# Layer norm's mean held to an upper place in TensorE's order, and layer 0's output projection begun with attention's half for two pairs of features

## The chip, the cores and the metric

The kernel runs on one core of one Trainium2 chip. The metric is the device time of one execution in microseconds (us); the time before is the median of three runs, 1300.79 us (1300.74 to 1301.24). The trace comes from one further execution, 1300.42 us long, of which the instructions span 1298.6 us. The engines are TensorE (PE: products, its weight loads are PEld), VectorE (DVE), ScalarE (ACT), GpSimd (POOL) and SyncE (SP, which issues most loads). They run their own queues in order and meet by semaphores.

## The reference, cut to what matters

A two-layer trunk works on 384 tokens (128 of a prompt, 256 of a sample) of 2048 features. Layer 0 is the one that changes:

```
h    = rms_norm(x, g) * (1 + sc) + sh             # sc, sh, gate: c @ w_mod
ga, gb, gate_a, q, k, v, gate_b = split(h @ w_in)
a = ga * sigmoid(gb)
a = depthwise_conv(a, conv_w) + conv_b            # 31 taps
a = silu(layer_norm(a, ln_g, ln_b)) * silu(gate_a)        # 1024 features
b = attention(norm(q), norm(k), v) * silu(gate_b)         # 1024 features
x = x + gate * (concat([a, b]) @ w_out)                   # 2048 x 2048
```

The layer norm goes over the 1024 features of `a`: it needs the mean over them, then the variance of what is left. Layer 1 (windowed attention beside a short gated convolution) follows, and a last RMS norm.

## The kernel before

Activations lie with features on the partitions: `mix` holds 16 tiles of 128 features by 384 tokens, tiles 0 to 7 for the convolution's half `a`, tiles 8 to 15 for attention's half `b`. Every matrix is multiplied in three products of split numbers: high x high, high x low, low x high. For that ScalarE casts a tile to its high part (`hhi` for activations, `whi` for weights, both at L283) and VectorE subtracts it for the low part (`hlo`, `wlo`, L284).

`proj_feat` (L394) makes one *pair* of feature tiles: two PSUM accumulators, over two units of 8 input tiles each. `feat_unit` (L374) runs one unit: two *halves* of 4 input tiles, each with its own weight load (512 KB on SyncE's queue), its split, and 24 products (L382) of 128x128 by 128x384. There are 5 accumulators (`pf`), 2 auxiliary PSUM buffers (`aux`: attention's `s_ps`, `pT_ps`, `o_ps`, the layer norm's `mean`, `rsl`, `rbl`), 6 raw weight buffers, and 3 each for `whi` and `wlo`.

The order in each engine's queue is set by a list scheduler that goes by a timeline of its own, within data dependencies and the few manual ones. A manual dependency of the kind NOSYNC says only that one instruction stands behind another on the same engine.

The end of layer 0, in the order of the program: attention; four pairs of `gate_a`; four pairs of `gate_b` (L781 to L797). After the first pair of `gate_b`, `ln_mean` (L751) sums the eight convolution tiles over the features with one product of TensorE (`mean`, L757), and `ln_center` subtracts it and gathers the squares (`lvar`). After the second pair `rsl` (L240) sums the squares over features, VectorE takes the inverse root (L229 to L234), TensorE spreads it (`rbl`, L256), `ln_out` multiplies (L773) and applies SiLU on ScalarE (L774). Last, L799 multiplies the result into tiles 0 to 7 of `mix`, and `out_proj` (L569) splits all 16 tiles and runs eight pairs (L588), tiles 0 to 7 before tiles 8 to 15 in each. The last two pairs are *held*: both do tiles 0 to 7, then both do the rest. Beside all this VectorE computes 64 dot products for layer 1's modulation rows (L207), whose operand `area` GpSimd's queue loads (L91) into buffers that are attention's until it ends.

Of the kernel before, what the change touches and what calls it, by code (L numbers as in the profile page):

```python
# [17 lines left out]
NOSYNC = mybir.DependencyInfo(mybir.DependencyClass.NoSync, mybir.DependencyReason.DATA)  # L18
# [4 lines left out]
T = 384  # L23
# [28 lines left out]
def trunk(ctx: ExitStack, tc: tile.TileContext, d: dict, o: dict):  # L52
# [10 lines left out]
    def aux(name):  # L63
        return ps_aux.tile([P, 512], F32, tag="aux", name=name)

    def acc(name):
        return ps_acc.tile([P, 512], F32, tag="acc", name=name)
# [24 lines left out]
        if order["hold"] is not None:  # L92
            tc.add_manual_dep(ins, order["hold"].name, SYNC, reason="side loads wait")

    order = {"last": None, "split": None, "hold": None}

    def sync_load(dst, src):
        ins = nc.sync.dma_start(dst, src).ins
# [4 lines left out]
    def load_w(w, k0, nk, f0, nf, raw=None):  # L103
        if raw is None:
            raw = wp.tile([P, nk, nf], F32, tag="raw", name="raw")
        sync_load(raw, w[:, k0:k0 + nk, f0:f0 + nf])
        return raw
# [174 lines left out]
    def split(dst_hi, dst_lo, src):  # L282
        nc.scalar.copy(dst_hi, src)  # L283
        order["split"] = nc.vector.tensor_tensor(dst_lo, src, dst_hi.bitcast(F32), ALU.subtract).ins  # L284

    def make_h(layer, k):
        if layer == 1:
            h = tmp.tile([P, T], F32, tag="wk", bufs=4, name="h1")
            for g, c0, c1 in GROUPS:
                nc.scalar.activation(h[:, c0:c1], x["T"][:, k, c0:c1], AF.Copy, scale=mods[layer, 1][:, k, g:g + 1])  # L290
            split(hhi[:, k, :T], hlo[:, k, :T], h)
            return
        for g, c0, c1 in GROUPS:
            a = mods[layer, 1][:, k, g:g + 1]
            nc.scalar.activation(hhi[:, k, c0:c1], x["T"][:, k, c0:c1], AF.Copy, scale=a)  # L295
            nc.vector.scalar_tensor_tensor(hlo[:, k, c0:c1], x["T"][:, k, c0:c1], a, hhi[:, k, c0:c1].bitcast(F32),
                                           ALU.mult, ALU.subtract)
# [20 lines left out]
    def pump():  # L318
        bg["due"] += bg["rate"]
        while bg["due"] >= 1.0 - 1e-6 and gemv_q:  # L320
            bg["due"] -= 1.0
            gemv_q.pop(0)()
# [23 lines left out]
    def load_split(w, k0, nk, nf):  # L346
        raw = load_w(w, k0, nk, 0, nf)
        hi = wp.tile([P, nk, nf], F32R, tag="whi", name="whi", bufs=NHI)
        lo = wp.tile([P, nk, nf], F32R, tag="wlo", name="wlo", bufs=NLO)
        split(hi, lo, raw)  # L350
        return hi, lo
# [22 lines left out]
    def feat_unit(pp, w, u, n, begin, end):  # L374
        for hf in range(2):
            hi, lo = load_split(w, 8 * u + 4 * hf, 4, 256)
            for j in range(2):
                fj = slice(j * P, (j + 1) * P)
                for i in range(4):
                    k = 8 * u + 4 * hf + i  # L380
                    for m, (x, y) in enumerate(((hi, hhi), (hi, hlo), (lo, hhi))):
                        ins = nc.tensor.matmul(pp[j][:, :n], lhsT=x[:, i, fj], rhs=y[:, k, :n],  # L382
                                               start=(begin and k % 8 == 0 and m == 0),
                                               stop=(end and k % 8 == 7 and m == 2)).ins
                        order["product"] = ins
            for _ in range(FILL):
                if fill_q:
                    fill_q.pop(0)()
        pump()

    def pair():
        return [acc(f"pf{j}") for j in range(2)]

    def proj_feat(w, evac, units=(0, 1), n=T):  # L394
        pp = pair()
        for u in units:
            feat_unit(pp, w, u, n, u == units[0], u == units[1])
        for j in range(2):
            evac(j, pp[j])
# [166 lines left out]
            return go  # L566
        return ev

    def out_proj(layer, w, mix, units, each, split_last=0, between=None):  # L569
        gate = mods[layer, 2]  # L570
        for k in (*range(8 * units[0], 8 * units[0] + 8), *range(8 * units[1], 8 * units[1] + 8)):
            split(hhi[:, k, :T], hlo[:, k, :T], mix[:, k, :])

        def ev(fb):
            def go(j, ps):
                f = 2 * fb + j
                if layer == 0:
                    s = tmp.tile([P, T], F32, tag="wk", bufs=4, name="go")
                    for g, c0, c1 in GROUPS:
                        nc.scalar.activation(s[:, c0:c1], ps[:, c0:c1], AF.Copy, scale=gate[:, f, g:g + 1])  # L580
                    nc.vector.tensor_tensor(x["T"][:, f, :], x["T"][:, f, :], s, ALU.add)
                else:
                    for g, c0, c1 in GROUPS:
                        nc.vector.scalar_tensor_tensor(x["T"][:, f, c0:c1], ps[:, c0:c1], gate[:, f, g:g + 1],
                                                       x["T"][:, f, c0:c1], ALU.mult, ALU.add)
                each(f)
            return go
        for fb in range(8 - split_last):  # L588
            proj_feat(w[fb], ev(fb), units)
        held = {fb: pair() for fb in range(8 - split_last, 8)}  # L590
        for fb, pp in held.items():
            feat_unit(pp, w[fb], units[0], T, True, False)
        if between:
            between()
        for fb, pp in held.items():
            feat_unit(pp, w[fb], units[1], T, False, True)
            for j in range(2):
                ev(fb)(j, pp[j])


    w0 = d["wf0"]
# [18 lines left out]
    for j, nf in enumerate(widths):  # L620
# [7 lines left out]
        last = j == len(widths) - 1  # L628
# [36 lines left out]
    mix = big.tile([P, KC, T], F32, tag="bigB", name="mix0")  # L665
# [85 lines left out]
    def ln_mean():  # L751
        av = tmp.tile([P, T], F32, tag="sacc", name="lsum", bufs=1)
        nc.vector.tensor_tensor(av, apad[:, 0, :T], apad[:, 1, :T], ALU.add)
        for c in range(2, 8):
            nc.vector.tensor_tensor(av, av, apad[:, c, :T], ALU.add)
        pm = aux("mean")
        ins = nc.tensor.matmul(pm[:, :T], lhsT=ones.broadcast_to([P, P]), rhs=av, start=True, stop=True).ins  # L757
        tc.add_manual_dep(ins, order["product"].name, NOSYNC, reason="not before its place")
        ln["m"] = tmp.tile([P, T], F32, tag="rb", name="mean", bufs=1)
        nc.scalar.activation(ln["m"], pm[:, :T], AF.Copy, scale=1.0 / CW)  # L760

# [20 lines left out]
    for fb in range(4):  # L782
        proj_feat(w0[12 + fb], evb(2 * fb))
        if fb == 0:
            ln_mean()
            for c in range(8):
                ln_center(c)
        if fb == 1:
            drain(gemv_q)
            ring["slots"] = []  # L790
            x["T"] = big.tile([P, KC, T], F32, tag="bigA", name="xT2")
            side_load(x["T"], d["xT"])
            ln["r"] = rstd_rows(rstd_cols([ln["v"]], CW, "rsl", order["product"]), "rbl")
            for c in range(8):
                ln_out(c)
            shifts.append(mod_rows(1, 0, 3, vring, ln["out"]))
            scales = [mod_rows(1, 1, j, vring, ln["out"]) for j in (1, 2, 3)]  # L797
# [5 lines left out]
    def each(f):  # L803
        square(f)
        if f in SCALE_AT:
            scales.pop(0)()
            if f == SCALE_AT[1]:
                for done in shifts:
                    done()
    def ahead():  # L810
        drain(gemv_q)
        for k in range(8):
            make_h(1, k)
    out_proj(0, d["w_out0"], mix, (0, 1), each, 2, ahead)


    for k in range(8, KC):
# [6 lines left out]
    mix = big.tile([P, KC, T], F32, tag="bigB", name="mix1")  # L824
# [101 lines left out]
    def each(f):  # L926
# [8 lines left out]
        if f % 4 == 1 and f > 4:  # L935
            q = f // 4 - 1
            nc.scalar.copy(y[0][:, 0, 512 * q:512 * q + 512], y_block(q, 0, after=False))
    out_proj(1, d["w_out1"], mix, (1, 0), each)
    rs2 = rstd_cols([av, *tail], D, "rs2")
    mid = [y_block(q, 1, acc) for q in range(3)]  # L940
# [96 lines left out]
```

## Time and profile before

| what | us |
|---|---|
| median of three runs | 1300.79 |
| the profiled execution | 1300.42 |
| its span of instructions | 1298.6 |
| TensorE busy | 1257.6 |
| VectorE busy | 884.9 |
| ScalarE busy | 564.6 |

The span is read as one chain: work that ended last, followed back to what released it. A row of a timeline gives start and duration; where an engine sat idle before, the bracket names who ended the wait. Products overlap in the array, so a product's duration is about twice the distance to the next; the sums go by the distance. The names in a row are the program's, without buffer numbers.

### The profile page before, as it was taken

To read this page: it belongs to the slowest core of one execution; us is meant where nothing else is said; L and a number is where in the kernel's file an instruction comes from. 1 tells how busy PE (TensorE), PEld (TensorE's weight loads), DVE (VectorE), ACT (ScalarE), POOL (GpSimd) and SP (SyncE) were. 2 spreads that over 40 slices of the span, in tenths; PEclk is the share of its full clock that TensorE was granted. 3 is DMA by queue.
4 is the path that set the end of the run, shared out by engine and by line. 5 is a ranking of instruction groups with operands and counts; after the bars stand their busy time and mean duration, and the time that the engine had idled before them with its cause. 6 is when DMAs were issued, how large, how long until landed. Compare 5 with 4: busy or idle time off the path is not lost.

```text
span 1298.6 us, 17795 instructions
## 1 busy us (share of the span) xinstructions
PE 1257.6 (97%) x6856; PEld 1116.1 (86%) x6856; DVE 884.9 (68%) x1507; ACT 564.6 (43%) x989; POOL 96.3 (7%) x137
## 2 busy tenths in 40 slices
PE   6999999999999999599999999999999999999997
PEld 3566676888978799499999988899999999999997
DVE  2244688998989975999976942354443599994443
ACT  3345432664465655433464632254444423343322
POOL 0211100000000000111100000000000011101110
PEclk9999999999999999799999999999999999999999
DMA  9989987787554344387743444333333578844422
GB/s 367 401 305 356 342 318 289 301 321 250 188 201 146 116 163 154 108 266 255 251 155 119 129 130 125 120 120 115 100 97 106 166 259 271 267 148 129 130 65 97
DMA packets 67620, 257.97 MB, mean 199 GB/s; under 512 B 7056, under 2 KB 11408, under 8 KB 59984
## 3 DMA queue, kind: packets, MB, share of 16 engines
q1 hardware_dynamic: 54736, 203.51, 45.4%
q0 software_dynamic: 12656, 53.23, 12.0%
q8 instruction: 53, 0.87, 0.3%
q14 instruction: 31, 0.25, 0.1%
q10 hardware_dynamic: 144, 0.10, 0.0%
HBM read 253.15 MB, written 3.67 MB: 198 GB/s over the span
## 4 chain that ended last, share of the span: by engine, by line
PE 96%; DVE 2%; DMA 1%; ACT 0%; issue 0%; SPq 0%; DVEq 0%; ACTq 0%
PE pf L382 68%; PE pt L361 10%; PE q L612 6%; PE gv L139 5%; PE s_ps L505 2%; PE o_ps L530 2%; PE pT_ps L526 1%; DMA ring<-in_mod_w 1%; PE y_ps L921 1%; PE gv L172 0%; PE qT_ps L491 0%; PE gv L676 0%; DVE mix L799 0%; DVE apad L773 0%; DVE area L207 0%
## 5 line engine op out<-in xcount | busy, mean ns | idle before, releaser
L382 PE MATMUL pf<-hhi,whi 128*128 128x384 f32 (+1 forms) x1664 | 568.9, 342 | 10.9 <-ACT hhi L283 10.6
L382 PE MATMUL pf<-hlo,whi 128*128 128x384 f32 (+1 forms) x1664 | 570.9, 343 | 5.0 <-DVE hlo L284 5.0
L382 PE MATMUL pf<-hhi,wlo 128*128 128x384 f32 (+1 forms) x1664 | 565.7, 342 | 1.2 <-DVE wlo L284 1.2
L284 DVE TENSOR_TENSOR wlo<-raw,whi 128x1024 fp32r<-128x1024 f32 x256 | 313.0, 1224 | 285.5 <-ACT whi L283 280.6
L283 ACT CAST whi<-raw 128x1024 fp32r<-128x1024 f32 x256 | 268.3, 1050 | 475.1 <-PE pf L382 267.4
L382 PEld LDWEIGHTS pf<-hhi,whi 128*128 128x128 f32 x1664 | 313.6, 189 | 31.9 <-issue 14.6
L382 PEld LDWEIGHTS pf<-hhi,wlo 128*128 128x128 f32 x1664 | 313.7, 189 | 12.2 <-issue 4.7
L382 PEld LDWEIGHTS pf<-hlo,whi 128*128 128x128 f32 x1664 | 314.1, 189 | 10.8 <-DVE hlo L284 5.5
L207 DVE CUSTOM_DVE_ANT_0 area<-area,crow 128x1024 f32<-128x1024 f32 x128 | 151.3, 1218 | 4.9 <-PE o_ps L530 4.4
L702 DVE SCALAR_TENSOR_TENSOR cv<-apad,cw,cv 128x399 f32<-128x399 f32 x240 | 138.7, 628 | 0.0
L361 PE MATMUL pt<-wlo,hhi 128*128 128x512 f32 x192 | 75.8, 395 | 0.0
L361 PE MATMUL pt<-whi,hhi 128*128 128x512 f32 x192 | 75.4, 396 | 0.0
L361 PE MATMUL pt<-whi,hlo 128*128 128x512 f32 x192 | 74.1, 395 | 0.0
L91 POOL DMA_DIRECT2D area<-in_modT x64 | 33.9, 531 | 457.6 <-DVE sm L207 223.8
L276 POOL TENSOR_TENSOR sacc<-sacc,sqf 128x384 f32<-128x384 f32 x28 | 33.5, 1196 | 176.4 <-ACT sqf L275 175.6
L361 PEld LDWEIGHTS pt<-whi,hhi 128*128 128x128 f32 x192 | 36.0, 188 | 11.0 <-ACT hhi L308 1.7
L612 PE MATMUL q<-whi,hhi 128*128 128x512 f32 x96 | 41.1, 428 | 4.4 <-ACT hhi L295 4.4
L361 PEld LDWEIGHTS pt<-whi,hlo 128*128 128x128 f32 x192 | 35.9, 188 | 10.0 <-DVE wlo L284 1.7
L139 PE MATMUL gv<-ring,cst 128*32 128x512 f32 (+1 forms) x288 | 35.6, 582 | 8.6 <-DMA ring<-in_mod_w 7.7
L361 PEld LDWEIGHTS pt<-wlo,hhi 128*128 128x128 f32 x192 | 36.1, 188 | 9.1 <-issue 0.8
L513 ACT ACTIVATE pr<-s_ps,nm 128x384 f32<-128x384 f32 (+1 forms) x48 | 24.4, 509 | 44.2 <-DVE nm L512 34.4
L612 PE MATMUL q<-wlo,hhi 128*128 128x512 f32 x96 | 40.5, 422 | 0.0
(186 smaller groups left out, 1005.9 us busy)
## 6 DMA issues: line engine op xcount, KB each, us to landing
raw<-in_wf SPq DMA_DIRECT2D x144, 512.0 KB, 4.5
ring<-in_mod_w SPq DMA_DIRECT2D x32, 1024.0 KB, 7.0
raw<-in_w_out SPq DMA_DIRECT2D x64, 512.0 KB, 4.1
area<-in_modT POOLq DMA_DIRECT2D x64, 512.0 KB, 5.2
lent<-in_mod_w SPq DMA_DIRECT2D x20, 1024.0 KB, 4.9
raw<-in_wq SPq DMA_DIRECT2D x32, 512.0 KB, 8.7
raw<-in_wt SPq DMA_DIRECT2D x24, 512.0 KB, 3.6
lent<-in_modT POOLq DMA_DIRECT2D x8, 1024.0 KB, 8.2
```

The source lines that it names most:

```text
L91: ins = nc.gpsimd.dma_start(dst, src).ins
L139: nc.tensor.matmul(ps[32 * g:32 * g + 32, :nf], lhsT=stat(k), rhs=raw[:, i % raw.shape[1], :], start=(k < 4), stop=(k >= KC - 4))
L207: ins = nc.vector.tensor_tensor_reduce(out=raw if g else junk, in0=raw, in1=crow[:, g, h * n:(h + 1) * n], scale=1.0, scalar=0.0, op0=ALU. ...
L276: eng.tensor_tensor(av, av, s, ALU.add)
L283: nc.scalar.copy(dst_hi, src)
L284: order["split"] = nc.vector.tensor_tensor(dst_lo, src, dst_hi.bitcast(F32), ALU.subtract).ins
L361: nc.tensor.matmul(pp[t], lhsT=x[:, k, tt], rhs=y[:, i, :], start=(k == 0 and n == 0), stop=(k == KC - 1 and n == 2))
L382: ins = nc.tensor.matmul(pp[j][:, :n], lhsT=x[:, i, fj], rhs=y[:, k, :n], start=(begin and k % 8 == 0 and m == 0), stop=(end and k % 8 == ...
L505: nc.tensor.matmul(ps, lhsT=mix[:, h0 + h, t * P:(t + 1) * P], rhs=kT[:, kv, c0:c0 + nk * P], start=True, stop=True)
L530: nc.tensor.matmul(po, lhsT=v[:, slots[j], kv * HD:(kv + 1) * HD], rhs=pT[:, j, :], start=(j == 0), stop=(j == nk - 1))
L612: nc.tensor.matmul(pq[b][t], lhsT=x[:, k, tt], rhs=y[:, 0, 512 * b:512 * b + 512], start=(k == 0 and n == 0), stop=(k == KC - 1 and n == 2))
L702: nc.vector.scalar_tensor_tensor(st["o"], apad[:, c, j:j + CVW], cw[:, c, j:j + 1], st["o"], ALU.mult, ALU.add)
```

## The change

`order` gets two entries: a count of halves issued, and a mark `must`. `ln_mean` now sets the mark: the product of the mean has to stand in front of the first product of the fifth half behind it, that is in front of the third pair of `gate_b`. In `out_proj` the code for held pairs becomes a function, `by_halves`, which is also used at the beginning (`split_first`). Layer 0 calls it with units (1, 0): tiles 8 to 15 first. So the first two pairs both do attention's half (8 halves of weights in the first four of which only tiles 8 to 15 are read), then both do the convolution's half; pairs 2 to 5 go tiles 8 to 15, then 0 to 7; the last two, with the units turned round, stay as they were. The sums and the products are the same.

```diff
--- before.py
+++ after.py
@@ -92,7 +92,7 @@
         if order["hold"] is not None:
             tc.add_manual_dep(ins, order["hold"].name, SYNC, reason="side loads wait")
 
-    order = {"last": None, "split": None, "hold": None}
+    order = {"last": None, "split": None, "hold": None, "must": None, "halves": 0}
 
     def sync_load(dst, src):
         ins = nc.sync.dma_start(dst, src).ins
@@ -374,6 +374,7 @@
     def feat_unit(pp, w, u, n, begin, end):
         for hf in range(2):
             hi, lo = load_split(w, 8 * u + 4 * hf, 4, 256)
+            order["halves"] += 1
             for j in range(2):
                 fj = slice(j * P, (j + 1) * P)
                 for i in range(4):
@@ -382,6 +383,9 @@
                         ins = nc.tensor.matmul(pp[j][:, :n], lhsT=x[:, i, fj], rhs=y[:, k, :n],
                                                start=(begin and k % 8 == 0 and m == 0),
                                                stop=(end and k % 8 == 7 and m == 2)).ins
+                        if order["must"] and order["must"][1] == order["halves"]:
+                            tc.add_manual_dep(ins, order["must"][0].name, NOSYNC, reason="not behind this place")
+                            order["must"] = None
                         order["product"] = ins
             for _ in range(FILL):
                 if fill_q:
@@ -566,7 +570,7 @@
             return go
         return ev
 
-    def out_proj(layer, w, mix, units, each, split_last=0, between=None):
+    def out_proj(layer, w, mix, units, each, split_first=0, split_last=0, between=None):
         gate = mods[layer, 2]
         for k in (*range(8 * units[0], 8 * units[0] + 8), *range(8 * units[1], 8 * units[1] + 8)):
             split(hhi[:, k, :T], hlo[:, k, :T], mix[:, k, :])
@@ -585,17 +589,21 @@
                                                        x["T"][:, f, c0:c1], ALU.mult, ALU.add)
                 each(f)
             return go
-        for fb in range(8 - split_last):
+
+        def by_halves(fbs, units, between=None):
+            held = {fb: pair() for fb in fbs}
+            for fb, pp in held.items():
+                feat_unit(pp, w[fb], units[0], T, True, False)
+            if between:
+                between()
+            for fb, pp in held.items():
+                feat_unit(pp, w[fb], units[1], T, False, True)
+                for j in range(2):
+                    ev(fb)(j, pp[j])
+        by_halves(range(split_first), units)
+        for fb in range(split_first, 8 - split_last):
             proj_feat(w[fb], ev(fb), units)
-        held = {fb: pair() for fb in range(8 - split_last, 8)}
-        for fb, pp in held.items():
-            feat_unit(pp, w[fb], units[0], T, True, False)
-        if between:
-            between()
-        for fb, pp in held.items():
-            feat_unit(pp, w[fb], units[1], T, False, True)
-            for j in range(2):
-                ev(fb)(j, pp[j])
+        by_halves(range(8 - split_last, 8), units[::-1], between)
 
 
     w0 = d["wf0"]
@@ -756,6 +764,7 @@
         pm = aux("mean")
         ins = nc.tensor.matmul(pm[:, :T], lhsT=ones.broadcast_to([P, P]), rhs=av, start=True, stop=True).ins
         tc.add_manual_dep(ins, order["product"].name, NOSYNC, reason="not before its place")
+        order["must"] = (ins, order["halves"] + 5)
         ln["m"] = tmp.tile([P, T], F32, tag="rb", name="mean", bufs=1)
         nc.scalar.activation(ln["m"], pm[:, :T], AF.Copy, scale=1.0 / CW)
 
@@ -811,7 +820,7 @@
         drain(gemv_q)
         for k in range(8):
             make_h(1, k)
-    out_proj(0, d["w_out0"], mix, (0, 1), each, 2, ahead)
+    out_proj(0, d["w_out0"], mix, (1, 0), each, 2, 2, ahead)
 
 
     for k in range(8, KC):
```

What the scheduler makes of it, at three places. On TensorE, at the end of attention 0: the last query block's transposes (`pT_ps`), its output (`o_ps`) and the layer norm's `mean`, among the products of the second pair of `gate_b` (`pf_3872` is the last accumulator of it) and the third (`pf_4146`, `pf_4147`). Before, around the mean:

```order
L382 MATMUL pf_4146<-hhi,whi 128x384
L382 MATMUL pf_4146<-hlo,whi 128x384
L382 MATMUL pf_4146<-hhi,wlo 128x384
L530 MATMUL o_ps<-pT,kv 128x512
L757 MATMUL mean<-lsum,ones 128x384
L382 MATMUL pf_4147<-hhi,whi 128x384
L382 MATMUL pf_4147<-hlo,whi 128x384
L382 MATMUL pf_4147<-hhi,wlo 128x384
```

In the change, at the same product of `pf_3872` as before:

```order
L383 MATMUL pf_3872<-hlo,whi 128x384
L383 MATMUL pf_3872<-hhi,wlo 128x384
L530 MATMUL pT_ps<-ident,pr 128x128 x12
L534 MATMUL o_ps<-pT,kv 128x512 x3
L765 MATMUL mean<-lsum,ones 128x384
L383 MATMUL pf_4146<-hhi,whi 128x384
L383 MATMUL pf_4146<-hlo,whi 128x384
L383 MATMUL pf_4146<-hhi,wlo 128x384
```

The mean moves up by 65 rows, to the front of the third pair; since it takes one of the two auxiliary buffers in turn, the attention rows that use them earlier (12 transposes and 3 products of `o_ps`, before strewn among the products down to the mean) move up with it. Then come 85 products up to `rsl`, 38 from there to `rbl`, and 69 from `rbl` to the output projection.

On VectorE, from the layer norm's multiplication by the inverse root (`apad<-apad,rb`) to the splits of `mix` into low parts. `ISA area` and `ISA sm` are one dot product for layer 1. Before:

```order
L773 TENSOR_TENSOR apad<-apad,rb 128x384 x8
L565 TENSOR_TENSOR mix_1217<-mix_1217,sg 128x384
L207 ISA area,sm_4046<-area,crow 128x1024
L207 ISA sm_4046 128x1
L284 TENSOR_TENSOR hlo<-mix_1217,hhi 128x384 x3
L799 TENSOR_TENSOR mix_1217<-mix_1217,apad 128x384 x7
L207 ISA area,sm_4046<-area,crow 128x1024
L207 ISA sm_4046 128x1
L207 ISA area,sm_4046<-area,crow 128x1024
L207 ISA sm_4046 128x1
L799 TENSOR_TENSOR mix_1217<-mix_1217,apad 128x384
L284 TENSOR_TENSOR hlo<-mix_1217,hhi 128x384 x8
```

In the change:

```order
L782 TENSOR_TENSOR apad<-apad,rb 128x384 x8
L207 ISA area,sm_4046<-area,crow 128x1024
L207 ISA sm_4046 128x1
L808 TENSOR_TENSOR mix_1217<-mix_1217,apad 128x384 x4
L284 TENSOR_TENSOR wlo<-raw,whi 128x1024
L808 TENSOR_TENSOR mix_1217<-mix_1217,apad 128x384
L207 ISA area,sm_4046<-area,crow 128x1024
L207 ISA sm_4046 128x1
L207 ISA area,sm_4046<-area,crow 128x1024
L207 ISA sm_4046 128x1
L808 TENSOR_TENSOR mix_1217<-mix_1217,apad 128x384 x3
L284 TENSOR_TENSOR hlo<-mix_1217,hhi 128x384 x5
```

The multiplication, the dot products and the products into `mix` stand as they did; a weight split has come between, the gate product is gone from here to a later place, and the first row of `hlo` in the change holds attention's tiles 8, 9 and 10 and the convolution's 0 and 1. Behind these 12 rows follow `wlo`, three `hlo` (tiles 11, 2, 3), two dot products, the gate product of tile 14, and `hlo` of tiles 12, 13 and 4.

On TensorE, where the output projection begins (`pf_4443` and `pf_4444` are its first pair, `pf_4445` and `pf_4446` its second). Before:

```order
L382 MATMUL pf_4275<-hlo,whi 128x384
L382 MATMUL pf_4275<-hhi,wlo 128x384
L256 MATMUL rbl<-diag,ones 128x128 x3
L382 MATMUL pf_4443<-hhi,whi 128x384
L382 MATMUL pf_4444<-hhi,whi 128x384
L382 MATMUL pf_4443<-hlo,whi 128x384
L382 MATMUL pf_4443<-hhi,wlo 128x384
L382 MATMUL pf_4443<-hhi,whi 128x384
```

In the change, nine products into the projection:

```order
L383 MATMUL pf_4443<-hhi,wlo 128x384
L383 MATMUL pf_4443<-hhi,whi 128x384
L383 MATMUL pf_4444<-hlo,whi 128x384
L383 MATMUL pf_4444<-hhi,wlo 128x384
L383 MATMUL pf_4444<-hhi,whi 128x384
L383 MATMUL pf_4445<-hhi,whi 128x384
L383 MATMUL pf_4445<-hlo,whi 128x384
L383 MATMUL pf_4446<-hhi,whi 128x384
L383 MATMUL pf_4446<-hlo,whi 128x384
```

Before, `rbl` is the last thing in front of the projection, and the first pair stands alone; in the change the first 96 products are those of two pairs on tiles 8 to 15, mixed. SyncE's loads and GpSimd's queue stand in the same order as before, but for the output stores at the very end.

## Rows read from the trace of the kernel before

**Rows 1.** TensorE's waits over the span: engine, line, releaser: us, times, longest.
```profile
PE pf L382 <- ACT hhi L283: 10.6, 1, 10.6
...
PE pf L382 <- DVE hlo L284: 5.0, 1, 5.0
```

**Rows 2.** Timeline of TensorE from 481 us: start, duration, engine, line, operation, count, idle before.
```profile
482.21 0.34 PE L382 MATMUL pf<-hhi,whi 128*128 128x384 f32 x1
...
521.10 0.93 PE L256 MATMUL rbl<-diag,ones 128*128 128x128 f32 x6
532.65 1.01 PE L382 MATMUL pf<-hhi,whi 128*128 128x384 f32 x2 [10.62 <-ACT hhi L283]
538.61 0.69 PE L382 MATMUL pf<-hlo,whi 128*128 128x384 f32 x1 [4.96 <-DVE hlo L284]
...
541.66 0.39 PE L382 MATMUL pf<-hlo,whi 128*128 128x384 f32 x1
```

**Rows 3.** Timeline of VectorE (DVE), 478 to 545 us, columns as in Rows 2.
```profile
498.00 3.84 DVE L763 TENSOR_TENSOR apad<-apad,mean 128x384 f32<-128x384 f32 x8 [2.00 <-ACT mean L760]
...
514.25 0.15 DVE L246 TENSOR_SCALAR rsl<-rsl 128x3 f32<-128x3 f32 x1
...
515.44 0.16 DVE L232 TENSOR_TENSOR nt<-ny 128x3 f32<-128x3 f32 x1
...
520.75 0.68 DVE L255 TENSOR_SCALAR diag<-ident,rsl 128x128 f32<-128x128 f32 x3
522.18 1.23 DVE L284 TENSOR_TENSOR wlo<-raw,whi 128x1024 fp32r<-128x1024 f32 x1 [0.75 <-ACT whi L283]
...
524.73 3.83 DVE L773 TENSOR_TENSOR apad<-apad,rb 128x384 f32<-128x384 f32 x8
...
528.95 1.22 DVE L207 CUSTOM_DVE_ANT_0 area<-area,crow 128x1024 f32<-128x1024 f32 x1
...
537.54 3.83 DVE L284 TENSOR_TENSOR hlo<-mix,hhi 128x384 fp32r<-128x384 f32 x8
```

**Rows 4.** Chain of waits, 480 to 545 us: start, us until the next link, link.
```profile
490.98 0.44 PE pT_ps L526 x4
491.41 1.72 PE o_ps L530 x4
...
496.80 0.65 PE mean L757 x2
497.44 15.60 PE pf L382 x89
513.04 0.56 PE rsl L240 x6
```

**Rows 5.** Windows: busy time of PE, PEld, DVE, ACT, POOL; granted clock; DMA share; GB/s.
```profile
14.00:18.00 4.00, 3.03 (x7) 2.45 (x8) 2.93 (x7) 1.65 (x5) 0.00 (x0) 1.00 1.11 350
...
48.00:50.00 2.00, 2.00 (x7) 1.54 (x6) 1.15 (x4) 0.30 (x1) 0.00 (x0) 0.50 0.99 406
...
539.00:541.00 2.00, 2.00 (x7) 2.00 (x7) 2.00 (x6) 0.00 (x0) 1.65 (x1) 0.50 0.13 51
```

**Rows 6.** Timeline of ScalarE (ACT), 478 to 545 us, columns as in Rows 2.
```profile
481.12 2.14 ACT L521 ACTIVATE pr<-pr,den 128x384 f32<-128x384 f32 x4 [0.24 <-DVE den L519]
483.17 1.03 ACT L283 CAST whi<-raw 128x1024 fp32r<-128x1024 f32 x1
486.89 1.08 ACT L527 COPY pT<-pT_ps 128x512 f32<-128x512 f32 x2 [2.69 <-PE pT_ps L526]
```

**Rows 7.** Timeline of TensorE in the first stage, columns as in Rows 2.
```profile
14.97 0.79 PE L612 MATMUL q<-whi,hhi 128*128 128x512 f32 x1 [2.19 <-ACT hhi L295]
...
45.87 0.50 PE L612 MATMUL q<-whi,hhi 128*128 128x512 f32 x1 [2.20 <-ACT hhi L295]
```

**Rows 8.** Timeline of GpSimd (POOL), 420 to 545 us, columns as in Rows 2.
```profile
497.09 1.57 POOL L91 DMA_DIRECT2D area<-in_modT  x3 [46.31 <-PE o_ps L530]
```

**Rows 9.** The page: DMA issues, count, size, median us from issue to landing.
```profile
area<-in_modT POOLq DMA_DIRECT2D x64, 512.0 KB, 5.2
```

## The prediction, made before the run

> **What bounds the kernel now.** I read the page's chain first: TensorE carries nearly all of it, so time is gained only where TensorE stops or runs slowly. Its waits by releaser show where: in the middle of the kernel there are only two of note, 10.6 us on ScalarE's `hhi` and 5.0 us on VectorE's `hlo`, each a single wait [rows 1]. The timeline of TensorE puts both between the layer norm's broadcast at 521.10 and the output projection [rows 2]: two products begin at 532.65, the third at 538.61. Behind that TensorE runs to the last sums without a wait of note. The chain of waits there goes through VectorE: inverse root, eight multiplications at 524.73, dot products, products into `mix`, low parts [rows 3]. So the projection waits for the layer norm, whose tiles 0 to 7 it reads first, and the layer norm started at 498.00, when the mean was there [rows 3, 4].
>
> What the stop costs: six records of the broadcast take 0.56 us as the six of `rsl` do [rows 4], so products could go on at 521.66; 538.61 less 521.66 is 16.95, less two products done in between, 0.35, leaves 16.6. A product takes 15.60 / 89 = 0.175 us [rows 4]. After the stop nine steps take 541.66 - 538.61 = 3.05 us instead of 1.58 [rows 2]; the granted clock there is 0.50, the 1.2 GHz level [rows 5]. That adds 1.5. All that can go is 18.1 us.
>
> **The change part by part.** No instruction is added or taken away: all terms are places in queues.
>
> *The mean moves up, and attention's tail with it.* In both kernels the product of 482.21 [rows 2] is the first of the third gate pair. In the change 12 transposes, 3 products of `o_ps` and the mean stand in front of it: 3 x 0.44 + 3 x 0.86 + 0.65 = 4.55 us of work [rows 4], which before lay among the next 60 products. It cannot run through. The last softmax scaling ends at 483.2, and behind it on ScalarE a weight cast runs to 484.2 [rows 6]; only then come the copies of the transposes, 0.54 each [rows 6]. With two buffers the third group of transposes waits for the first copy, and `o_ps` for the second: 484.2 + 1.1 = 485.3. Then 2.6 for `o_ps`, 0.65 for the mean: 488.5. The gate products start 6.3 us later than before, 4.55 of which is work that is no longer in their way: **new idle 1.75 us**. Every gate product, its weight splits and their loads are queued behind it; three splits are ahead, so none runs dry.
>
> *The layer norm moves up.* The mean ends at 488.5 instead of 497.45. ScalarE first copies `o_ps`, then the mean, so centring starts at about 489.2 instead of 498.00. It and the squares share VectorE with two weight splits and end near 499.7. TensorE's place for `rsl` is 85 products behind the mean: 488.5 + 14.9 = 503.4, so the place decides, not the squares. `rsl` takes 0.56. Twelve small steps at 0.2 (seven of them stand between 514.25 and 515.44) and the diagonals' 0.7 [rows 3] end at 507.2; the broadcast's place, 38 products behind `rsl`, is 510.6. It ends at 511.2, its copy on ScalarE, taken like the copies of [rows 6], at 512.0. The eight multiplications start at **512.2 instead of 524.73: 12.5 us earlier**. The 69 products from the broadcast to the projection end at 511.2 + 12.1 = 523.2.
>
> *The projection starts with attention's half.* On VectorE's queue there stand, from 512.2: eight multiplications 3.75, a dot product 1.15, four products into `mix` 1.9, a weight split 1.15, one product 0.45, two dot products 2.3, three products 1.4 (distances from [rows 3]: 0.47 for 128x384, 1.15 for 128x1024). That is 12.1: 524.3. The low part of tile 8 is done at 524.85. TensorE has had two products that need only high parts and stood since 523.55: **wait 1.3 us**. It then has 28 products before the first that reads tile 12's low part: until 529.75. VectorE meanwhile does five low parts 2.35, a weight split 1.15, three low parts 1.4, two dot products 2.3, a gate product and tile 12's low part 1.0: 532.5. **Wait 2.75 us**. The other tiles of the first 96 products come in time, by my count with 0.1 us to spare at tile 14: the 96 end at 544.1. Before, product 97 began at 541.66 + 85 x 0.175 = 556.5. That is 12.4 us, and the balance of waits says the same: 18.1 - 1.75 - 1.3 - 2.75 = 12.3.
>
> *What is late next.* The layer norm's tiles are split by 537 and read from 544.1: the cover of 96 products holds. VectorE then has per half of 4.2 us one weight split and two dot products, 3.45 us, and about 0.5 for sums: it follows, as before, and all of its work moved with it. Of five accumulators the first pair and the last gate pair hold four, so one of the second pair's two comes free only when ScalarE has read the gate pair, some 2 us after its last product; about ten of the projection's products stand in front. Taken at nothing, bounds 0 and 1.
>
> *Loads.* SyncE's and GpSimd's queues keep their order. The `area` loads, which waited for attention's end at 497.09 [rows 8], can go 9 us earlier; they take 5.2 us [rows 9], and the dot products in front of tile 8 stand more than 20 us behind.
>
> *The clock.* Two waits of nearly one length on TensorE stand in the first stage, 2.19 us at 14.97 and 2.20 us at 45.87 [rows 7]. Behind the second the granted clock was 0.50 from 48 to 50; around the first it was 1.00, the 2.4 GHz level, from 14 to 18 [rows 5]. So my 2.75 us may or may not lower it, and if it does, 1.5 us are lost as after the old stop. I take none, since 28 products at full speed stand ahead of that wait; 1.5 stays in the range. [...]
>
> Sum: 1300.4 - 12.3 = 1288.1 for an execution like the profiled one. That one is 0.4 under the median shown, so I say **1288.3 us**.
>
> **Rivals.**
> - *The new waits throttle the clock.* For: 45.87 in [rows 7]. Against: 14.97 in the same rows. 1289.8 with one, 1291.3 with both.
> - *VectorE's queue becomes the bound by more than I counted.* Tile 12's low part stands behind two dot products and two weight splits, tile 14's behind four dot products; any late operand stops all that follow. For: in the sum above VectorE is never idle, and my spare time at tile 14 is 0.1 us. If the fourth load from the new order, issued when its buffer falls free, landed in 9 us instead of 5.2 [rows 9], or the chain began 3 to 4 us later, each would add that much: 1292.
> - *The cover is better than counted.* If ScalarE takes the attention copies ahead of time or VectorE's waits fall where TensorE has other pairs to do, the 5.8 us of new waits shrink; at nothing left, 1282.5. Against: the queues are in order, and the sums leave no choice.
> - *Slower.* One mechanism: TensorE, stopped at short intervals over the first two pairs, stays at 1.2 GHz for all of their 192 products. Each then costs 0.32 - 0.175 = 0.145 more: 27.8 us, less the 2.75 wait that slower products would hide: 1313. It decides from 85 products on, where the gain of 12.3 is eaten. Against: after 541.66 full distance came back in nine products, with VectorE just as far behind.
> - *That it doesn't do what it says* is shut out by the order: the mean stands 65 rows up, and tiles 8 to 15 are the first the projection reads.
>
> **How the numbers follow.** The forecast's own range, 1286.5 to 1289.5, has 0.5; the clock 0.2; VectorE's queue 0.13; better cover 0.1; the slow clock 0.03; what I overlooked 0.04, half of it within 0.2% of before (what a measurement of this kernel can tell from no change: 1298.2 to 1303.4). The range goes from 1285 (half of the better cover) to 1293 (all but the worst of VectorE's case). Faster 0.93, same 0.04, slower 0.03.
>
> **What would show it.** Right: the mean's product ends near 488.5, centring starts near 489, the eight multiplications near 512; TensorE's wait on `hhi` is gone, and on `hlo` there are one of 1 to 2 and one of 2 to 4 us; TensorE is at its 97th product of the projection near 544. Wrong: a wait of over 3 us at attention's tail (a sum of ScalarE's queue that I missed); a wait on `area` or `wlo` past 545 (VectorE as bound); granted clock 0.50 for more than 4 us between 523 and 545.

## The result, and the profile after

The changed kernel takes **1288.73 us** (median of four runs, 1288.58 to 1289.09), the kernel before beside it 1301.01 (1300.74 to 1301.28): a ratio of 0.9906, 95% interval 0.9889 to 0.9923. The profiled execution took 1288.71 us, its instructions span 1286.9.

TensorE's waits, 478 to 700 us (engine, line, releaser: us, times, longest); they stand where [rows 1] had 10.6 and 5.0:

```profile
PE pf L383 <- DVE hlo L284: 3.9, 3, 2.5
PE pT_ps L530 <- ACT pT L531: 1.0, 1, 1.0
```

Its timeline over the same stretch, the counterpart of [rows 2]:

```profile
484.32 0.66 PE L530 MATMUL pT_ps<-ident,pr 128*128 128x128 f32 x4 [0.98 <-ACT pT L531]
...
487.48 0.81 PE L765 MATMUL mean<-lsum,ones 128*128 128x384 f32 x2
...
510.35 0.83 PE L256 MATMUL rbl<-diag,ones 128*128 128x128 f32 x6
...
524.75 0.44 PE L383 MATMUL pf<-hlo,whi 128*128 128x384 f32 x1 [1.12 <-DVE hlo L284]
...
532.39 0.44 PE L383 MATMUL pf<-hlo,whi 128*128 128x384 f32 x1 [2.49 <-DVE hlo L284]
...
544.09 0.34 PE L383 MATMUL pf<-hhi,whi 128*128 128x384 f32 x1
...
671.86 0.45 PE L383 MATMUL pf<-hlo,whi 128*128 128x386 f32 x1 [0.26 <-DVE hlo L284]
```

The stop of 16 us is gone. Three waits on low parts are left, 1.12, 2.49 and, at the start of layer 1, 0.26; and 0.98 at attention's tail. The projection's 97th product, the first of the convolution's half, begins at 544.09.

VectorE's timeline, the counterpart of [rows 3]:

```profile
488.85 3.84 DVE L772 TENSOR_TENSOR apad<-apad,mean 128x384 f32<-128x384 f32 x8 [3.81 <-ACT mean L769]
...
512.06 3.83 DVE L782 TENSOR_TENSOR apad<-apad,rb 128x384 f32<-128x384 f32 x8
515.81 1.22 DVE L207 CUSTOM_DVE_ANT_0 area<-area,crow 128x1024 f32<-128x1024 f32 x1
...
520.44 1.22 DVE L207 CUSTOM_DVE_ANT_0 area<-area,crow 128x1024 f32<-128x1024 f32 x1
...
524.13 2.43 DVE L284 TENSOR_TENSOR hlo<-mix,hhi 128x384 fp32r<-128x384 f32 x5
...
529.02 1.22 DVE L207 CUSTOM_DVE_ANT_0 area<-area,crow 128x1024 f32<-128x1024 f32 x1
...
531.78 1.49 DVE L284 TENSOR_TENSOR hlo<-mix,hhi 128x384 fp32r<-128x384 f32 x3
```

Centring starts at 488.85, the eight multiplications at 512.06. The low parts of tiles 8 to 11 begin at 524.13, behind three dot products (one at 515.81, two from 520.44); tile 12's stands first in the group of 531.78, behind two more, so it is done at 531.78 + 0.57 = 532.35, and TensorE goes on at 532.39.

The chain of waits from the mean to the sums of squares (as [rows 4]):

```profile
487.64 0.65 PE mean L765 x2
488.29 14.87 PE pf L383 x85
503.16 0.56 PE rsl L240 x6
```

The place of `rsl`, 85 products behind the mean, decides when the inverse root starts; the layer norm's squares were ready at 499.3.

ScalarE at attention's tail (as [rows 6]), the loads of the dot products' operand on GpSimd (as [rows 8]), and two windows behind the longest wait (as [rows 5]):

```profile
480.72 2.13 ACT L525 ACTIVATE pr<-pr,den 128x384 f32<-128x384 f32 x4 [0.25 <-DVE den L523]
482.76 1.03 ACT L283 CAST whi<-raw 128x1024 fp32r<-128x1024 f32 x1
483.69 1.06 ACT L531 COPY pT<-pT_ps 128x512 f32<-128x512 f32 x2
```

```profile
487.94 1.57 POOL L91 DMA_DIRECT2D area<-in_modT  x3 [37.57 <-PE o_ps L534]
```

```profile
531.00:533.00 2.00, 0.61 (x3) 0.61 (x4) 2.00 (x6) 0.51 (x1) 0.08 (x1) 1.00 0.59 129
533.00:535.00 2.00, 2.00 (x14) 1.96 (x13) 2.00 (x4) 0.09 (x1) 0.00 (x0) 1.00 0.37 143
```

The softmax scaling starts 0.40 us earlier than in [rows 6]: the whole trace is ahead by that much before the change begins. The loads of the dot products' operand start 9.15 us earlier than in [rows 8]. The copies of the transposes stand behind the weight cast, as forecast. The granted clock stays at 1.00, the 2.4 GHz level, behind the wait of 2.49 us.

### The profile page after: what moved, and what is told of

Read it like the earlier page. It is cut to its first block, busy times and chain, and to the rows that moved or that the text cites. A ratio compares the mean times of both kernels' runs of the same rounds, so it can differ in the third digit from the quotient of the medians.

```text
span 1286.9 us, 17791 instructions
## 1 busy us (share of the span) xinstructions
PE 1256.1 (98%) x6856; PEld 1113.9 (87%) x6856; DVE 885.5 (69%) x1507; ACT 564.9 (44%) x989; POOL 96.4 (7%) x137
## 4 chain that ended last, share of the span: by engine, by line
PE 95%; DVE 2%; ACT 1%; issue 1%; DMA 1%; SPq 0%; DVEq 0%; ACTq 0%
PE pf L383 67%; PE pt L361 10%; PE q L620 6%; PE gv L139 5%; PE o_ps L534 2%; PE s_ps L509 2%; PE pT_ps L530 1%; DMA ring<-in_mod_w 1%; PE y_ps L930 1%; PE gv L172 0%; PE qT_ps L495 0%; DVE wlo L284 0%; DVE hlo L284 0%; ACT whi L283 0%; PE gv L684 0%
```

## The experiments

The theory: the places of the low parts in VectorE's queue, counted from the layer norm's inverse root on, set TensorE's waits at the start of the projection, and attention's 96 products hide the rest. Against it stand an earlier layer norm alone, the cover alone, the clock, and VectorE's work as a whole. All were timed beside the kernel before, at 1300.5 to 1300.8 in each set.

**One part alone: the mean.** `out_proj` is called as before.

```diff
-        by_halves(range(8 - split_last, 8), units[::-1], between)
+        by_halves(range(8 - split_last, 8), units, between)
...
-    out_proj(0, d["w_out0"], mix, (1, 0), each, 2, 2, ahead)
+    out_proj(0, d["w_out0"], mix, (0, 1), each, 0, 2, ahead)
```

> The mean is held to its upper place, but the output projection begins as before: tiles 0 to 7 in every pair, no pair held at the start. Theory (the place of each low part in VectorE's queue sets the waits): that queue is nearly the changed kernel's, with the low parts of tiles 0 to 7 among those of tiles 8 to 11. TensorE waits 2.2 us for tile 0, 0.9 for tile 2, 1.4 for tile 4 and 2.0 for tile 5, 6.5 in all instead of the 3.9 of the changed kernel: 1291.3 us (1290 to 1293). Rival 'the layer norm's start decides alone': as the changed kernel, 1288.7. Rival 'the cover decides': with no products that are free of the layer norm nearly all of the gain is lost, 1298 or more. Rival 'the clock': each wait of about 2 us halves the clock for 3 us behind it, 1.5 more for each of two, 1294.3.

Measured 1292.69 (1290.12 to 1294.15), ratio 0.9936 (0.9924 to 0.9949): the median is in the forecast's range, and two of the five runs are nearer to the rival with the clock, 1294.3. The profiled execution is the fastest of the five. TensorE's waits, and a window behind the first:

```profile
524.98 0.44 PE L383 MATMUL pf<-hlo,whi 128*128 128x384 f32 x1 [2.05 <-DVE hlo L284]
...
531.69 0.45 PE L383 MATMUL pf<-hlo,whi 128*128 128x384 f32 x1 [0.68 <-DVE hlo L284]
...
534.70 0.44 PE L383 MATMUL pf<-hlo,whi 128*128 128x384 f32 x1 [1.68 <-DVE hlo L284]
```

```profile
526.00:528.00 2.00, 2.00 (x8) 2.00 (x8) 2.00 (x4) 0.22 (x1) 0.54 (x1) 0.50 0.02 4
```

The wait for tile 0 came as counted (2.05). Behind it the clock fell to 0.50, and products at half speed let VectorE catch up: the 0.9 forecast for tile 2 is gone, tile 4's 1.4 became 0.68, tile 5's 2.0 became 1.68. Here half clock is not added to the waits behind it, it takes their place. The early layer norm alone gives 8.0 of the 12 us by the medians, 6.5 to 10.6 by single runs.

**The other part alone: the projection.** The line that sets `must` is taken out.

```diff
-        order["must"] = (ins, order["halves"] + 5)
```

> The mean stays where it was (60 products lower); the output projection begins with attention's half for two pairs. Theory: no idle time at attention's tail (1.0 to 1.75 us less), the low parts of tiles 8 to 11 now stand ahead of the layer norm's eight multiplications, and the layer norm's broadcast stands behind the projection's first 12 products. TensorE does 48 products of the projection from 521.1 while VectorE still works on the layer norm; tile 12 is split by 530.2, tile 15 by 538.9, tile 0 by 540.5; waits of about 0.4 and 1.1 us, product 97 near 540.4 instead of 544.1 in the changed kernel: 1284.4 us (1283 to 1287), faster than the changed kernel without the mean's new place. Rival 'the layer norm's start decides': as late as before, 1298 to 1301. Rival 'the parts add': between, about 1294.

Measured 1290.66 (1289.46 to 1292.81), ratio 0.9929 (0.9916 to 0.9943): 10 us gained, but 2 us slower than the changed kernel, where I had it 4 faster. VectorE's timeline, then TensorE's only wait of that stretch and the window behind it:

```profile
515.97 1.49 DVE L284 TENSOR_TENSOR hlo<-mix,hhi 128x384 fp32r<-128x384 f32 x3
...
518.59 0.55 DVE L284 TENSOR_TENSOR hlo<-mix,hhi 128x384 fp32r<-128x384 f32 x1
...
523.62 3.83 DVE L781 TENSOR_TENSOR apad<-apad,rb 128x384 f32<-128x384 f32 x8
...
537.57 0.56 DVE L284 TENSOR_TENSOR hlo<-mix,hhi 128x384 fp32r<-128x384 f32 x1
```

```profile
538.18 0.44 PE L383 MATMUL pf<-hlo,whi 128*128 128x384 f32 x1 [1.96 <-DVE hlo L284]
```

```profile
541.00:543.00 2.00, 2.00 (x8) 2.00 (x8) 2.00 (x5) 0.01 (x1) 0.00 (x0) 0.51 0.54 182
```

Up to there the count held: tile 8 to 11's low parts stand ahead of the eight multiplications, tile 15 is split at 538.13, and its wait is 1.96 instead of the two of 0.4 and 1.1. What I had left out is half clock behind it, ten products at 0.32 instead of 0.175, 1.5 us, and what follows at the start of layer 1. A cast on ScalarE there, and a piece of the chain of waits (start, us until the next link):

```profile
667.69 1.04 ACT L283 CAST whi<-raw 128x1024 fp32r<-128x1024 f32 x1 [2.14 <-issue]
```

```profile
667.69 1.04 ACT whi L283
668.74 0.42 ACT sqf L275
669.16 2.08 ACT h L290 x6
671.24 0.41 ACT hhi L283
```

The cast of a weight's high part runs at 667.69, and six activations and a cast stand behind it on ScalarE. TensorE waits 1.00 and then 1.93, with half clock behind. The weight had not come late from memory: there are six raw buffers, and each load here is issued 0.03 us behind the end of the low part that stands six weights before its own. So the load of this cast is the one of 645.34, 22 us ahead, and loads land 4.7 us after their issue (the profile's median). What held the cast for 2.14 us this trace does not name ("issue"). In dots_later and p6_dots, further down, ScalarE stands idle before the same cast for 2.11 and 2.10 us, and there the profile names a product of TensorE; so one of the three buffers for high parts is the likely reason, which is not shown for this run.

The longer wait on tile 15 (0.5), half clock twice (about 1.5 each) and the two waits at layer 1 (2.9) make 6.4, and the forecast was 6.3 us too low. VectorE's last dot product ran at 674.7 here, at 656.8 in the changed kernel. So the two parts, 8.0 and 10.0 alone, 12.3 together, don't add: they shorten the same stop, and the second alone brings a loss of its own at layer 1.

**Is it the dot products?** 16 of the 64 are left out, in proj_only and, as a control, in the changed kernel; the rows that they would give are filled with 1.0.

```diff
-            scales = [mod_rows(1, 1, j, vring, ln["out"]) for j in (1, 2, 3)]
+            scales = [mod_rows(1, 1, j, vring, ln["out"]) for j in (1, 2)]
+            scales.append(lambda: nc.vector.memset(mods[1, 1][:, 12:16, :], 1.0))
```

> proj_only once more (mean at its old place, projection begun with attention's half), but 16 of the 64 dot products are left out, those of the last four scale tiles of layer 1, which are filled with 1.0 instead. Proj_only reached layer 1 2.8 us ahead of the changed kernel and lost 2.9 us of waits and 1.5 us of half clock at 668 to 676. Theory: VectorE's dot products (they ended at 675.8 there) were late, since layer 1's first tiles wait for the scales that they give. VectorE's queue up to 543 is the same, so the wait of 2.0 us on tile 15 and the half clock behind it stay; the waits at 668 are gone: 1290.4 - 4.4 = 1286.0 us (1285 to 1287.5). Rival 'weights': the waits at 668 are on casts of weights that came late from memory, and stay: 1290.5.

> The changed kernel without the last 16 of the 64 dot products (layer 1's last four scale tiles are filled with 1.0 instead), as a control for proj_fewer. Theory: in the changed kernel VectorE's later load is just hidden (its last dot product ended at 658.0; TensorE waits 0.3 us at the start of layer 1), so leaving dot products out behind 560 brings at most that: 1288.4 us (1288.0 to 1288.8); the waits of 1.1 and 2.5 us stay. Rival 'fewer dot products make any of these kernels faster' (less VectorE work, fewer loads): 1286 or less.

Measured 1285.84 (1285.24 to 1286.19), ratio 0.9886 (0.9871 to 0.9901), and 1288.33 (1288.04 to 1288.97), 0.9906 (0.9889 to 0.9923). All that is left of TensorE's waits in the first, 478 to 700 us:

```profile
PE pf L383 <- DVE hlo L284: 2.0, 1, 2.0
```

Both times came out as the theory had them: without the 16, proj_only's loss at layer 1 is gone, and the changed kernel keeps its time. In proj_only the dot products start 12 us later, with the layer norm (527.84 against 515.81); in the changed kernel they are hidden. How they act is not shown. The waits were for casts, and not for the scales that the theory named. And leaving instructions out also changes the order that the scheduler makes: ScalarE's timeline of proj_fewer has six activations `h` in front of the cast that ran at 667.69 in proj_only (here at 668.52), and proj_only has them behind it.

```profile
662.46 2.17 ACT L290 ACTIVATE h<-xT,mod 128x128 f32<-128x128 f32 x6
...
668.52 1.03 ACT L283 CAST whi<-raw 128x1024 fp32r<-128x1024 f32 x1
```

One thing more follows from the two. With 16 dot products left out of both, the kernel with the mean at its old place is 2.5 us faster than the one with the mean moved up (1285.84 against 1288.33). So next to the new start of the projection, the early mean pays through what happens at layer 1, and not at the projection's start, where the waits are not shorter for it (0.98, 1.12 and 2.49 against 1.96 and 1.5 of half clock).

**The cover halved.** No pair is held at the start.

```diff
-    out_proj(0, d["w_out0"], mix, (1, 0), each, 2, 2, ahead)
+    out_proj(0, d["w_out0"], mix, (1, 0), each, 0, 2, ahead)
```

> The changed kernel, but the first two pairs are not held: each pair does tiles 8 to 15 and then 0 to 7, so 48 products instead of 96 are free of the layer norm. Theory: VectorE's queue is the changed kernel's up to tile 13. The waits for tile 8 (1.1 us) and tile 12 (2.8) stay; then only 12 products lie before tile 14, whose low part is done at 540.1: a third wait of 5.5 us. 1294.3 us (1293 to 1296). Rival 'the cover does nothing once the layer norm is early': as the changed kernel, 1288.7. Rival 'the clock': half clock behind the longest wait, 1.5 us more, 1295.8.

Measured 1296.29 (1295.24 to 1297.25), ratio 0.9967 (0.9956 to 0.9979). TensorE's timeline:

```profile
524.71 0.44 PE L383 MATMUL pf<-hlo,whi 128*128 128x384 f32 x1 [1.12 <-DVE hlo L284]
...
532.36 0.44 PE L383 MATMUL pf<-hlo,whi 128*128 128x384 f32 x1 [2.85 <-DVE hlo L284]
...
540.20 0.69 PE L383 MATMUL pf<-hlo,whi 128*128 128x384 f32 x1 [5.48 <-DVE hlo L284]
```

The three waits were forecast as 1.1, 2.8 and 5.5. The clock fell to 0.50 inside the last one, so the time is just above the forecast's range and nearer to the rival with half clock, 1295.8. So the second pair's 48 products are worth 7.6 us: the third wait, 0.4 more at tile 12, and half clock.

**The dot products out of the way.** They may stand only behind tile 15's low part.

```diff
             split(hhi[:, k, :T], hlo[:, k, :T], mix[:, k, :])
+            if layer == 0 and k == 15:
+                shifts.append(mod_rows(1, 0, 3, vring, order["split"]))
+                scales.extend(mod_rows(1, 1, j, vring, order["split"]) for j in (1, 2, 3))
...
-            shifts.append(mod_rows(1, 0, 3, vring, ln["out"]))
-            scales = [mod_rows(1, 1, j, vring, ln["out"]) for j in (1, 2, 3)]
```

> The changed kernel, but the dot products of the last four groups of modulation rows may stand only behind tile 15's low part on VectorE. Theory: three dot products (3.5 us) go from before tile 8's low part, two more from before tile 12's. Tile 8 is split by 522.3, tile 11 by 525.8, tile 12 by 528.6: of the 3.9 us of waits on low parts 0.2 stay, 1285.0 us (1284.3 to 1287). Rival 'VectorE is the bound': it is busy nearly without a break from 511 to 660, the dot products are only put off and TensorE waits for weights' low parts later, 1288 to 1291.

Measured **1285.78** (1285.61 to 1285.92), ratio 0.9887 (0.9873 to 0.9900). TensorE's waits, 478 to 700 us:

```profile
PE pT_ps L530 <- ACT pT L531: 1.0, 1, 1.0
PE pf L383 <- ACT whi L283: 1.0, 1, 1.0
PE pf L383 <- DVE wlo L284: 0.3, 1, 0.3
```

No wait on a low part of the projection is left: 3.6 us of waits hung on five dot products' places. The rival is right in part: 0.28 us is waited for a weight's low part at 669.1; another 0.95 at 667.8 is for a high part, which is ScalarE's. The next run leaves 16 dot products out of this kernel, the same ones as above.

> dots_later without the last 16 of the 64 dot products (layer 1's last four scale tiles are filled with 1.0 instead). Dots_later waited 0.95 us for a weight's high part and 0.28 for its low part at 668 to 669. Theory: these waits come from the dot products that were put off; with fewer they go: 1285.8 - 1.2 = 1284.6 us (1284.2 to 1285.1). Rival: they come from the order of the last products and the three buffers of high parts, and stay, as turned has them with its last dot product at 663: 1285.8.

Measured 1284.66 (1284.02 to 1284.80), ratio 0.9876 (0.9862 to 0.9891); both waits are gone, as the theory had it. Weights late from memory are not the reason: in dots_later each load of this stretch is issued 18.6 us or more ahead of its cast. Whether VectorE's time is, or the order that the scheduler makes with fewer instructions, is not told apart.

**Other ways to the same 3.6 us.** In turned, the last pair of `gate_b` is turned, so that tiles 8 to 15 come free earlier; p6_turned2 also has the mean 24 products lower. p6_dots is dots_later with the mean 24 products lower and with `rsl` and `rbl` held to upper places on TensorE. The main lines, of turned and p6_turned2:

```diff
-        proj_feat(w0[12 + fb], evb(2 * fb))
+        proj_feat(w0[12 + fb], evb(2 * fb), (1, 0) if fb == 3 else (0, 1))
```

of p6_turned2 in addition:

```diff
-        order["must"] = (ins, order["halves"] + 5)
+        order["must"] = (ins, order["halves"] + 6)
```

and of p6_dots, where `must` is a list:

```diff
-        order["must"] = (ins, order["halves"] + 5)
+        order["must"].append((ins, order["halves"] + 6))
...
+            order["must"] += [(order["sum"], order["halves"] + 5), (order["spread"], order["halves"] + 6)]
```

> The changed kernel, but the last pair of gate_b takes its units the other way round, so that tiles 8 to 15 of the old activations are read for the last time 8.4 us before the projection begins. Theory: the low parts of tiles 8 to 11 then stand ahead of the layer norm's eight multiplications on VectorE, 12 and 13 just behind, with all dot products where they were. Both waits of the changed kernel (1.1 and 2.5) go; tile 14 is split by 536.1 where TensorE needs it at 536.4, tile 15 by 538.9 where it needs it at 538.6: 0.3 to 1 us of wait stays, 1285.4 us (1284.6 to 1287). Rival 'dot products are the bound': what is gained is waited for at the start of layer 1, 1287 to 1288.7. Rival 'the casts': ScalarE casts tiles 8 to 11 in front of the copy of the layer norm's broadcast and the chain starts 1 us later or more, 1286.5.

> turned with the mean one half (24 products) lower. Theory: the stop of 1.0 us at attention's tail goes and the projection starts 1.2 us earlier; the layer norm's multiplications start near 516 instead of 512.2, since the low parts of tiles 8 to 11 now stand among the steps of the inverse root; tile 14 is split at 536.5 and TensorE needs it at 535.2: 1.4 us of wait: 1285.0 us (1284 to 1287). The dot products start later by 3 to 4 us; rival 'dot products are the bound': 1 to 3 us are waited for at the start of layer 1, 1286 to 1288.

> dots_later with three places on TensorE moved: the mean one half (24 products) lower, the sums of squares (rsl) 72 products and the broadcast (rbl) 96 products behind it, instead of 85 and 123. Theory: attention's last transposes now lie among products and the 1.0 us stop at attention's tail goes, with some 0.2 of what is left there; the layer norm's multiplications still start 2.4 us earlier (509.7), a wait of 0.5 us for the broadcast is new; the dot products start 2.2 us earlier, so 0.3 to 1 of the 1.2 us waited at layer 1's start in dots_later stays: 1284.6 us (1283.8 to 1286). Rival 'the tail's stop only moves': the transposes wait for ScalarE anyway, 1285.8. Rival 'the broadcast': VectorE's chain is not done at the new place and TensorE stops there by 2 us, 1287.

Measured 1287.48 (1287.29 to 1287.51), ratio 0.9899 (0.9884 to 0.9913), for turned; 1286.65 (1286.42 to 1287.11), 0.9892 (0.9876 to 0.9909), with the mean lower; and **1285.38** (1285.22 to 1285.61), 0.9883 (0.9868 to 0.9898), for p6_dots. TensorE's waits in turned, then in p6_dots, 478 to 700 us:

```profile
PE pf L383 <- DVE wlo L284: 1.5, 2, 1.3
PE pf L383 <- ACT whi L283: 1.0, 1, 1.0
PE pT_ps L530 <- ACT pT L531: 1.0, 1, 1.0
```

```profile
PE pf L383 <- ACT whi L283: 1.0, 1, 1.0
PE pf L383 <- DVE hlo L284: 0.5, 1, 0.5
PE pf L383 <- DVE wlo L284: 0.3, 1, 0.3
```

Turned missed by 2.1: the waits on tiles are gone, but 1.25 us are waited at 536.08 for a weight's low part, which stands behind four low parts of tiles and two dot products and which I hadn't counted, and the 1.3 us at layer 1's start appear here too, though its last dot product started at 662.2; so they are not only a matter of dot products put off. p6_turned2 stays in its range, but 1.65 above the forecast: it waits 1.58 for a weight's low part, 0.48 for a tile, and 1.25 at layer 1, as its rival had it. In p6_dots attention's tail has no wait any more, and tile 12 costs 0.5. Its runs lie below all runs of the changed kernel. Against dots_later no difference is shown: its highest run equals the lowest of dots_later, 1285.61, the intervals overlap, and the kernel before beside it ran 0.2 us faster as well.

## Why the prediction was right

The forecast was 1288.3; 1288.73 was measured. By its steps (times of the trace; the trace's 0.4 us lead stands inside each):

- *Attention's tail*: mean forecast to end at 488.5, the third gate pair goes on at 488.29 (behind the mean's row of 487.48). Of the new idle, forecast at 1.75, the profile lists 0.98 as a wait on the copies; the rest lies between the transposes ahead of it.
- *Layer norm*: centring 489.2, measured 488.85; multiplications 512.2, measured 512.06, 12.7 earlier than in [rows 3]. The place of `rsl` decided, not the squares.
- *Waits at the start*: 1.3 and 2.75 forecast, 1.12 and 2.49 measured, on the tiles named. dots_later shows that they hang on the dot products, no_held that 96 products are needed.
- *Product 97*: forecast 544.1, measured 544.09. Tile 14's spare time of 0.1 us held: no wait there.
- *What was luck*: with the lead taken off, the mean, the centring, the multiplications and product 97 lie 0.05 to 0.4 us above the forecast; product 97 would begin at 544.5. That it agrees to 0.01 is chance.
- *Clock*: taken as not lowered, and so it was, behind 1.12 and behind 2.49. The reason that I gave, 28 products at full speed ahead of the wait, does not hold: in mean_only and proj_only it fell behind shorter waits, 2.05 and 1.96, with far more such products ahead. So this term was right by luck.
- *What I had wrong*: the 0.26 us at layer 1's start; and the rival "VectorE's queue becomes the bound", to which I gave 0.13. Up to 545 nothing of it showed; the place that I had not looked at is the start of layer 1, where proj_only lost 2.9 us and half clock to casts on ScalarE, a loss that goes when dot products are left out.

The balance: the medians lie 12.3 us apart, as forecast, the two profiled executions 11.7; and that includes the lead of 0.4. In the traces, TensorE's last group of products starts 12.06 us earlier (1285.61 before, 1273.55 after), so about 0.3 of the 12.4 at product 97 is lost up to there, 0.26 of it at layer 1's start. The last 0.35 is lost behind it, where the output stores stand in another order; how is not traced.

## What to carry to other kernels

Where an engine's queue is in order, list what stands ahead of the awaited instruction and add it up: in the changed kernel and with the cover halved, five waits forecast so came within 0.3 us, two of them read off the changed kernel's trace before. Where the count failed (proj_only, turned), TensorE waited for an instruction that I had not listed, a weight's cast or its low part. Two changes that shorten the same stop are not to be added; run each alone. And work that fills gaps is owed at a later deadline: what moves its start, or puts it behind something, has to be checked there too.

## What the hardware showed that I had not expected

Whether TensorE's clock falls does not go by the length of the wait alone. As in [rows 7], two waits of one length differ here: it fell to 0.50 behind waits of 1.96 us (proj_only, 538.18) and 2.05 us (mean_only, 524.98), before which TensorE had run without any wait for over 35 us. It stayed at 1.00 behind 2.49 us (the changed kernel, 532.39) and 2.85 us (no_held, 532.36), where a wait of 1.12 us lay 7.6 us earlier. A wait shortly before does not keep it up either: in proj_only a wait of 1.93 us ended at 671.69, 2.9 us behind the end of one of 1.00, and the clock was 0.50 from 674 to 676.

In three kernels with such a fall in their trace the runs scatter more: 4.0, 3.4 and 2.0 us between the lowest and the highest in mean_only, proj_only and no_held, against 0.2 to 0.9 in the kernels without one. The mean granted clock of every run goes with it: in mean_only 0.994 in the two slowest runs and 0.996 to 0.997 in the others, in proj_only 0.994 in the two slowest and 0.995 to 0.996 in the others, in no_held 0.991 in the two slowest and 0.994 in the others. But a fall alone does not make the scatter: proj_fewer has one, behind a wait of 1.95 us at 538.29, and its runs lie within 1.0 us, those of the kernel before, with its long stop, within 1.3.
